# Grouped scaling of attention outputs, queries and keys stored by parts, operands of products 64 bytes apart

## The chip, the cores and the metric

The kernel runs on one core of a Trainium2 chip. The metric is the device time of one execution in microseconds; the median of three runs stands for a kernel. TensorE (PE in the profile) multiplies, VectorE (DVE), ScalarE (ACT) and GpSimd (POOL) do the element-wise work, SyncE (SP) issues most DMA transfers. PEld is TensorE's load of the stationary operand, which overlaps the multiplication.

## The reference

Two layers of a diffusion backbone. 2048 latent tokens and 256 context tokens of width 1024 go through one input projection, three groups of heads, one output projection, and a mixture of 16 experts of which each chooses its tokens. Group A is windowed attention (6 query heads on 2 key heads, with a sink in the softmax), group B a gated short convolution, group C neighbourhood attention of 6 heads on a grid with a bias by relative position.

```
qa, ka, va, bx, bb, bc, qn, kn, vn = _split_last(h @ w_in[l], IN_SPLITS)
...
p_win, p_ctx, _ = joint_softmax([s_win, s_ctx, s_sink])
o = (jnp.einsum('bnkgqj,bnjkd->bnqkgd', p_win.astype(v.dtype), vw)
     + jnp.einsum('bnkgqj,bjkd->bnqkgd', p_ctx.astype(v.dtype), v_ctx))
...
s_nb = s_nb + jnp.transpose(bias, (1, 0, 2, 3, 4))[None].astype(jnp.float32)
p_nb, p_ctx = joint_softmax([s_nb, s_ctx])
...
mix = jnp.concatenate([o_a, o_b, o_c], axis=-1) @ w_out[l]
...
y = jnp.einsum('becf,efd->becd', jax.nn.silu(a) * u, w_down) * gate[..., None].astype(h.dtype)
```

All of it is float32. The kernel splits each operand into a high and a low part and adds three products (high by high, low by high, high by low).

## The kernel before

Each layer runs four phases one after the other: `phase_in` (input projection), `phase_att` (attention), `phase_out` (output projection, LayerNorm, router) and `phase_moe` (experts). Within a phase the instructions of all engines are written in the order of the program; the order of attention is a string of steps per member (`ORDERA`, `ORDERC`) in the loop over `mem`, with the epilogue of a block (`pv`, a generator) advanced a step at every "R". Loads of weights (L163) run ahead as a stream on SP.

Products outside attention: L627 to L629 and L805 to L807 in the input phase, L1317 in the output phase, L1828 to L1830 (gate, up) and L1865 to L1867 (down) with the experts. Where a tile lies in SBUF is set by the order in which pools are opened. The distance of the two operands' addresses in a partition, modulo 128 bytes, is 96 for L627 to L629, 32 for L805 to L807 and for L1317, 96 (layer 0) and 64 (layer 1) for L1828 to L1830, 64 (layer 0) and 32 (layer 1) for L1865 to L1867, and mostly 0 for the products of attention (L1061, L1062, L1166).

The input phase writes queries and keys to DRAM, high and low part, by head: QA, QC, KC as [head, part, 64, tokens], KA as [head, part, 64, tokens] for two heads. One SBUF tile of 128 partitions holds two heads, so every store is made in two halves of 64 partitions (L660, L749, L787, L788).

Attention works unit by unit: two A units (a key head each) and six C units (a head each). An A unit has 18 blocks in layer 0 and 16 in layer 1, of three members (the query heads); a C unit has four blocks of four members, and in layer 0 before them a short one (n = 4) of two members for the context. Per member: logits (L1061, L1062, PE), maximum and mask (L1083, DVE), exponential (L1091, ACT), transposes (PE) with copies (L1220, ACT; L1211, DVE), and per block the product with the values (L1166, PE). The epilogue of a block: copy (L1172, ACT), in A the sink's share (L1174 DVE, L1175 ACT, L1184 DVE), transposes (L1179), copy (L1182), reciprocal (L1186), sum (L1188), scaling (L1191, all DVE), and stores to MIXA (one) or MIXC (four, L1199).

SP issues for attention, in order: the key load of the next unit (`load_unit`, L951; in A units with the fifth block, in C units with the second; at the phase's start in two parts of 640 and 1664 columns), with it the values va or vx and, for C, toep (L964), from which POOL builds the bias tiles (L1025); three query loads for each block, three blocks ahead (L976, L980, L982); four value loads for each C block, two blocks ahead (L994); and the stores. Keys of one head lie together: high and low part, 128 rows of 9216 bytes, one behind the other, go to 128 partitions. toep reads 8 x 16 rows of 4032 bytes.

Of the kernel before, what the change touches and what calls it, by code (L numbers as in the profile page):

```python
# [7 lines left out]
F32 = mybir.dt.float32  # L8
F32R = mybir.dt.float32r
BF = mybir.dt.bfloat16  # L10
I32 = mybir.dt.int32
AF = mybir.ActivationFunctionType
# [9 lines left out]
TT = SEQ + CTX  # L22
# [202 lines left out]
def build(ctx, tc, t, out):  # L225
# [4 lines left out]
    const = ctx.enter_context(tc.tile_pool(name="const", bufs=1))  # L230
    dram = ctx.enter_context(tc.tile_pool(name="dram", bufs=1, space=DRAM))
# [10 lines left out]
    half = const.tile([128, 2], F32, name="half")  # L242
# [9 lines left out]
    slotc = const.tile([128, 2], F32, name="slotc")  # L252
# [18 lines left out]
    QA = dr("QA", [6, 2, 64, TT])  # L271
    KA = dr("KA", [2, 2, 64, TT])
    QC = dr("QC", [6, 2, 64, TT])
    KC = dr("KC", [6, 2, 64, TT])
# [230 lines left out]
    def phase_in(l):  # L505
# [5 lines left out]

        hT = {-1: [hp.tile([128, KD, 512], F32R, name=z) for z in ("hh", "hl")]}
# [102 lines left out]
        def gemm(c):  # L615
# [16 lines left out]
            def c_rest(f, pg):  # L632
# [25 lines left out]
                for a, z in enumerate((sh, sl)):  # L658
                    for b in range(2):
                        SY.dma_start(dst[2 * (f % 3) + b, a, :, tok + t0:tok + nt],  # L660
                                     z.bitcast(F32)[64 * b:64 * b + 64, t0:nt])
# [77 lines left out]
            def ctx_rest(f, pg):  # L739
# [7 lines left out]
                for a, z in enumerate((sh, sl)):  # L747
                    for b in range(2):
                        SY.dma_start((QA[l][2 * f + b] if f < 3 else KA[l][b])[a, :, 0:256], z.bitcast(F32)[64 * b:64 * b + 64])  # L749

            def a_rest(i, pg):
# [32 lines left out]
                for a, o in enumerate((qh, ql)):  # L784
                    for b in range(2):
                        z = o.bitcast(F32)[64 * b:64 * b + 64]
                        SY.dma_start(QA[l][b::2, a, :, tk].rearrange("f p n -> p f n"), z[:, 0:3, :])  # L787
                        SY.dma_start(KA[l][b, a, :, tk], z[:, 3, :])  # L788
# [107 lines left out]
    def phase_att(l):  # L896
        es = ExitStack()

        kp = es.enter_context(tc.tile_pool(name="at_k", bufs=2))
        qp = es.enter_context(tc.tile_pool(name="at_q", bufs=1))  # L900
        vwp = es.enter_context(tc.tile_pool(name="at_vw", bufs=3))
        op = es.enter_context(tc.tile_pool(name="at_o", bufs=6))
        mp = es.enter_context(tc.tile_pool(name="at_m", bufs=1))
        vp = es.enter_context(tc.tile_pool(name="at_v", bufs=2))
        sm = es.enter_context(tc.tile_pool(name="at_s", bufs=4))
        pp = es.enter_context(tc.tile_pool(name="at_p", bufs=3))
# [11 lines left out]
        biases = [None, bp.tile([128, BWID], F32, name="bias")]  # L918
# [11 lines left out]
        NM = len(mem)  # L930
# [1053 lines left out]
```

## Time and profile before

| | us |
|---|---|
| median of three runs | 4121.46 (4118.05 to 4125.27) |
| profiled execution | 4118.59 |
| its span | 4116.8, mean granted clock 0.960 |
| busy PE, DVE, ACT, POOL | 3801.8, 2899.2, 2007.7, 706.6 |

The page of the profile gives busy time and shares by engine, the groups of instructions by line, and the transfers; a window gives the same for a stretch; the timeline gives single instructions with their starts. Matmuls overlap, so that the mean of one in a group is longer than the step from one to the next; the step is read from the timeline.

### The profile page before, as it was taken

What the parts mean: (1) busy time and instruction counts of PE and PEld (TensorE: products, weight loads), DVE (VectorE), ACT (ScalarE), POOL (GpSimd) and SP (SyncE); (2) the same over time, 40 slices, a digit from 0 to 9 for tenths busy, and PEclk for the clock granted to TensorE, in tenths of its full rate; (3) what the DMA queues carried; (4) which work ended last, traced back from release to release, by engine and by line L of the source; (5) the groups of instructions that cost most, each with busy time, mean ns of one, the idle gap of its engine ahead of it and who ended that gap; (6) DMA issues with size and microseconds to landing.
All of it is one profiled execution on the core that took longest, in us unless ns stands there. A gap on an engine that the chain in (4) does not pass through costs nothing. (4 is left out here: it accounts for less than half of the span.)

```text
span 4116.8 us, 64178 instructions
## 1 busy us (share of the span) xinstructions
PE 3801.8 (92%) x22980; PEld 3241.1 (79%) x22980; DVE 2899.2 (70%) x5836; ACT 2007.7 (49%) x3918; POOL 706.6 (17%) x658
## 2 busy tenths in 40 slices
PE   7999999999898899999996999989998966999983
PEld 5877788888787378989985888888897855999972
DVE  6555558999677467767756766469996776777765
ACT  4344337988433044444434434359884332444453
POOL 0000000022123023233311000000221221222214
PEclk9999999999999999999998999999999977999996
DMA  7566665377643677777757766563676424888875
GB/s 227 172 201 206 191 191 143 94 177 175 216 162 122 201 246 219 218 217 216 209 164 225 228 196 188 171 166 107 149 177 225 162 105 153 243 248 255 248 240 184
DMA packets 768951, 785.81 MB, mean 191 GB/s; under 512 B 144912, under 2 KB 650520, under 8 KB 766584
## 3 DMA queue, kind: packets, MB, share of 16 engines
q1 hardware_dynamic: 732776, 657.53, 53.3%
q0 software_dynamic: 34704, 123.13, 10.8%
q8 instruction: 182, 2.98, 0.3%
q14 instruction: 137, 1.12, 0.1%
q10 hardware_dynamic: 1152, 1.05, 0.1%
HBM read 603.05 MB, written 178.48 MB: 190 GB/s over the span
## 5 line engine op out<-in xcount | busy, mean ns | idle before, releaser
L178 ACT CAST wh<-wraw 128x1024 fp32r<-128x1024 f32 x636 | 657.9, 1051 | 387.5 <-DMA wraw<-in_w_in 116.5
L186 DVE TENSOR_TENSOR wl<-wraw,wh 128x1024 fp32r<-128x1024 f32 x636 | 751.2, 1216 | 19.2 <-ACT wh L178 18.8
L1211 DVE TENSOR_TENSOR pl<-pt,ph 128x256 fp32r<-128x256 f32 (+2 forms) x792 | 360.7, 495 | 13.0 <-ACT ph L1220 7.9
L627 PE MATMUL gem<-hh,wh 128*128 128x512 f32 (+1 forms) x960 | 354.5, 369 | 0.0
L628 PE MATMUL gem<-hl,wh 128*128 128x512 f32 (+1 forms) x960 | 352.2, 367 | 0.0
L1091 ACT ACTIVATE p<-lg,mx 128x640 f32<-128x640 f32 (+3 forms) x408 | 332.0, 814 | 37.7 <-DVE mx L1083 36.4
L629 PE MATMUL gem<-hh,wl 128*128 128x512 f32 (+1 forms) x960 | 350.4, 365 | 0.0
L1220 ACT CAST ph<-pt 128x256 fp32r<-128x256 f32 (+2 forms) x792 | 309.5, 446 | 59.1 <-PE pt L1108 53.3
L1828 PE MATMUL pu<-xh,wh 128*128 128x288 f32 (+1 forms) x1024 | 304.6, 297 | 10.1 <-DVE sa L1656 10.1
L1828 PE MATMUL pa<-xh,wh 128*128 128x288 f32 (+1 forms) x1024 | 300.9, 294 | 0.9 <-DVE modc L419 0.9
L1061 PE MATMUL lg<-k,q 128*128 128x384 f32 (+2 forms) x768 | 280.1, 387 | 20.9 <-DMA maskA<-in_maskA 7.4
L1830 PE MATMUL pa<-xh,wl 128*128 128x288 f32 (+1 forms) x1024 | 296.9, 290 | 0.8 <-DVE wl L186 0.8
L1830 PE MATMUL pu<-xh,wl 128*128 128x288 f32 (+1 forms) x1024 | 296.4, 289 | 0.0
L1829 PE MATMUL pa<-xl,wh 128*128 128x288 f32 (+1 forms) x1024 | 294.4, 288 | 0.0
L1829 PE MATMUL pu<-xl,wh 128*128 128x288 f32 (+1 forms) x1024 | 294.1, 287 | 0.0
L1567 POOL DMA_INDIRECT xe<-H,ix x80 | 164.7, 2059 | 473.3 <-DVE ix L1562 398.2
L1062 PE MATMUL lg<-k,q 128*128 128x256 f32 x816 | 228.3, 286 | 0.4 <-ACT p L1091 0.4
L1690 POOL DMA_INDIRECT ACC<-y,ix x62 | 127.1, 2050 | 583.6 <-DVE y L1671 324.3
L1865 PE MATMUL py<-wh,gh 128*128 128x512 f32 x512 | 206.5, 403 | 17.3 <-ACT gh L1658 10.1
L805 PE MATMUL gem<-wh,hh 128*128 128x512 f32 x544 | 220.7, 406 | 0.0
L806 PE MATMUL gem<-wl,hh 128*128 128x512 f32 x544 | 217.3, 399 | 1.4 <-DVE wl L186 1.4
L807 PE MATMUL gem<-wh,hl 128*128 128x512 f32 x544 | 216.9, 399 | 0.0
(346 smaller groups left out, 9681.5 us busy)
## 6 DMA issues: line engine op xcount, KB each, us to landing
wraw<-in_w_in SPq DMA_DIRECT2D x160, 512.0 KB
wraw<-in_w_gate SPq DMA_DIRECT2D x128, 512.0 KB
wraw<-in_w_up SPq DMA_DIRECT2D x128, 512.0 KB
wraw<-in_w_down SPq DMA_DIRECT2D x128, 512.0 KB
wraw<-in_w_mod SPq DMA_DIRECT2D x88, 512.0 KB
vw<-VS SPq DMA_DIRECT2D x192, 128.0 KB
q<-QA SPq DMA_DIRECT2D x204, 96.0 KB
VS<-vs SPq DMA_DIRECT2D x36, 512.0 KB
```

Source lines behind the costliest of these rows:

```text
L178: self.nc.scalar.copy(h, self.raw[i])
L186: self.nc.vector.tensor_tensor(e[1], self.raw[i], e[0].bitcast(F32), op=ALU.subtract)
L627: P.matmul(pg[:, t0:nt], wh[:, cs_], hh[:, k, t0:nt], start=(k == 0), stop=False)
L628: P.matmul(pg[:, t0:nt], wh[:, cs_], hl[:, k, t0:nt], start=False, stop=False)
L629: P.matmul(pg[:, t0:nt], wl[:, cs_], hh[:, k, t0:nt], start=False, stop=(k == KD - 1))
L1061: P.matmul(pl[:, w0:512], q[:, x, m, :], win(k), start=(x == 0), stop=(x == 1))
L1091: S.activation(p[:, 0:768 - w0], rec["lg"][:, w0:768], AF.Exp, bias=st[b]["mx"][:, m:m + 1], scale=-1.0, accum_out=st[b]["ss"][:, m:m + 1])
L1211: V.tensor_tensor(view(st[b]["pl"]), src, view(st[b]["ph"].bitcast(F32)), op=ALU.subtract)
L1220: S.copy(view(st[b]["ph"]), src)
L1828: P.matmul(pp[f], wh[:, cs_], xh[:, kk, :], start=(kk == 0), stop=False)
L1829: P.matmul(pp[f], wh[:, cs_], xl[:, kk, :], start=False, stop=False)
L1830: P.matmul(pp[f], wl[:, cs_], xh[:, kk, :], start=False, stop=(kk == KD - 1))
```

## The change

First, the operands of the large products come to lie 64 bytes apart (modulo 128): small unused pools (`shift`) and a new order of the attention pools move the tiles, and the input phase drops a pair of tiles that it kept under index -1. Second, QA, QC, KC are laid out as [part, head, 64, tokens], and the two halves of a store become one transfer of 128 rows; queries are read from the new layout in the same shape. Third, the key loads: the two parts of a head now lie 884,736 elements (C) or 294,912 (A) apart, and the load's source is [2, 64, n]. Fourth, the outputs of up to four A blocks (two C blocks) go into one tile of 12 x 64 columns; sink's share, reciprocal and scaling are done once for the group, in A with the scaling on POOL, and the stores follow together: MIXA once per group, MIXC eight in a row. The reciprocal and the scaling of C stay on DVE. Two small constants share a tile.

On SP, in a C unit of layer 1 around the key load (k is the keys, q queries, vw and vx values; DMAHW0 to 7 are the eight lanes that a transfer must find free). Before:

```order
L951 DMA k<-KC_88 128x2304 [waits DMAHW1_49]
L958 DMA vx<-VS_90 128x2x128 [waits DMAHW2_49]
L964 DMA toep<-in_rpb 128x1x1008 [waits DMAHW3_49,Pool_49]
L1199 DMA MIXC_96<-o 8x16x64 [waits DMAHW4_49,DVE_49]
L1199 DMA MIXC_96<-o 8x16x64 [waits DMAHW5_49]
L1199 DMA MIXC_96<-o 8x16x64 [waits DMAHW6_49]
L1199 DMA MIXC_96<-o 8x16x64 [waits DMAHW7_49]
L982 DMA q_27373<-QC_86 64x8x64 [waits DMAHW0_49]
L982 DMA q_27373<-QC_86 64x8x64 [waits DMAHW1_49]
L982 DMA q_27373<-QC_86 64x8x64 [waits DMAHW2_49]
L994 DMA vw<-VS_90 32x8x128 [waits DMAHW3_49,PE_49]
```

After:

```order
L962 DMA k<-KC_87 128x1x2304 [waits DMAHW5_49]
L969 DMA vx<-VS_89 128x2x128 [waits DMAHW6_49]
L975 DMA toep<-in_rpb 128x1x1008 [waits DMAHW7_49,Pool_49]
L993 DMA q_26821<-QC_85 64x8x64 [waits DMAHW0_49]
L993 DMA q_26821<-QC_85 64x8x64 [waits DMAHW1_49]
L993 DMA q_26821<-QC_85 64x8x64 [waits DMAHW2_49]
L1005 DMA vw<-VS_89 32x8x128 [waits DMAHW3_49,PE_49]
L1005 DMA vw<-VS_89 32x8x128 [waits DMAHW4_49]
L1005 DMA vw<-VS_89 32x8x128 [waits DMAHW5_49]
L1005 DMA vw<-VS_89 32x8x128 [waits DMAHW6_49]
L1229 DMA MIXC_95<-o 8x16x64 [waits DMAHW7_49,DVE_49]
```

The stores that stood behind toep come later and in eights; q and vw stand right behind toep, and the third vw needs the lane of k. The key load's shape is now 128x1x2304, where it was 128x2304.

On DVE, one A block in the middle of a unit (lg logits, mx maximum, pl low part, ss sum, rs reciprocal, o output). Before:

```order
L1191 TENSOR_TENSOR o<-o,rs 128x192
L1174 TENSOR_TENSOR rs<-sinks,mx 128x3
L1211 TENSOR_TENSOR pl<-pt,ph 128x3x128
L1211 TENSOR_TENSOR pl<-pt,ph 128x2x128
L1083 ISA lg,mx<-lg,maskA,sinks 128x640
L1083 ISA mx 128x1
L1184 TENSOR_TENSOR ss<-ss,rs 128x3
L1211 TENSOR_TENSOR pl<-pt,ph 128x3x128
L1211 TENSOR_TENSOR pl<-pt,ph 128x2x128
L1186 RECIPROCAL rs<-ss 128x3
L1083 ISA lg,mx<-lg,maskA,sinks 128x640
```

After, the block that ends a group:

```order
L1191 TENSOR_TENSOR rs<-sinks,mx 128x12
L1241 TENSOR_TENSOR pl<-pt,ph 128x3x128
L1241 TENSOR_TENSOR pl<-pt,ph 128x2x128
L1097 ISA lg,mx<-lg,maskA,sinks 128x640
L1097 ISA mx 128x1
L1206 TENSOR_TENSOR ss<-ss,rs 128x12
L1241 TENSOR_TENSOR pl<-pt,ph 128x3x128
L1241 TENSOR_TENSOR pl<-pt,ph 128x2x128
L1209 RECIPROCAL rs<-ss 128x12
L1097 ISA lg,mx<-lg,maskA,sinks 128x640
L1097 ISA mx 128x1
L1211 TENSOR_TENSOR o<-pt,o 128x192
```

The scaling has left DVE, and L1174, L1184 and L1186 (now L1191, L1206, L1209) work on 12 columns once for four blocks; the three other blocks have only the sum (now L1211) of them. On POOL, from the start of attention in layer 0 to its first bias additions, after:

```order
L1217 TENSOR_TENSOR o<-o,rs 128x768 x4
L1217 TENSOR_TENSOR o<-o,rs 128x384
L1217 TENSOR_TENSOR o<-o,rs 128x768 x3
L1024 MEMSET bias 128x2048
L1028 MEMSET va 128x256 x3
L1036 TENSOR_TENSOR va<-maskC,toep 128x384
```

There the scaling stands alone, up to the first bias tiles.

The diff, with line numbers left out:

```diff
+
+    def shift(es, n):
+
+        pool = es.enter_context(tc.tile_pool(name="shift", bufs=1))
+        pool.tile([128, n // 4], F32, name="shift")
...
-    half = const.tile([128, 2], F32, name="half")
+    halves = const.tile([128, 4], F32, name="half")
+    half, slotc = halves[:, 0:2], halves[:, 2:4]
...
-    QA = dr("QA", [6, 2, 64, TT])
+
+    QA = dr("QA", [2, 6, 64, TT])
     KA = dr("KA", [2, 2, 64, TT])
-    QC = dr("QC", [6, 2, 64, TT])
-    KC = dr("KC", [6, 2, 64, TT])
+    QC = dr("QC", [2, 6, 64, TT])
+    KC = dr("KC", [2, 6, 64, TT])
...
-        hT = {-1: [hp.tile([128, KD, 512], F32R, name=z) for z in ("hh", "hl")]}
+        hT = {}
...
                 dst = QC[l] if f < 3 else KC[l]
                 for a, z in enumerate((sh, sl)):
-                    for b in range(2):
-                        SY.dma_start(dst[2 * (f % 3) + b, a, :, tok + t0:tok + nt],
-                                     z.bitcast(F32)[64 * b:64 * b + 64, t0:nt])
+                    SY.dma_start(dst[a, 2 * (f % 3):2 * (f % 3) + 2, :, tok + t0:tok + nt], z.bitcast(F32)[:, t0:nt])
...
-                    for b in range(2):
-                        SY.dma_start((QA[l][2 * f + b] if f < 3 else KA[l][b])[a, :, 0:256], z.bitcast(F32)[64 * b:64 * b + 64])
+                    SY.dma_start((QA[l][a, 2 * f:2 * f + 2] if f < 3 else KA[l][a])[:, :, 0:256], z.bitcast(F32))
...
-                    for b in range(2):
-                        z = o.bitcast(F32)[64 * b:64 * b + 64]
-                        SY.dma_start(QA[l][b::2, a, :, tk].rearrange("f p n -> p f n"), z[:, 0:3, :])
-                        SY.dma_start(KA[l][b, a, :, tk], z[:, 3, :])
+                    SY.dma_start(QA[l][a, :, :, tk].rearrange("(f b) p n -> (b p) f n", b=2), o.bitcast(F32)[:, 0:3, :])
+                    SY.dma_start(KA[l][a, :, :, tk], o.bitcast(F32)[:, 3, :])
...
         kp = es.enter_context(tc.tile_pool(name="at_k", bufs=2))
+        pp = es.enter_context(tc.tile_pool(name="at_p", bufs=3))
+        op = es.enter_context(tc.tile_pool(name="at_o", bufs=3))
+        shift(es, 64)
         qp = es.enter_context(tc.tile_pool(name="at_q", bufs=1))
-        vwp = es.enter_context(tc.tile_pool(name="at_vw", bufs=3))
-        op = es.enter_context(tc.tile_pool(name="at_o", bufs=6))
+        shift(es, 64)
+        bsp = es.enter_context(tc.tile_pool(name="at_bias", bufs=1))
+        tp = es.enter_context(tc.tile_pool(name="at_toep", bufs=2))
         mp = es.enter_context(tc.tile_pool(name="at_m", bufs=1))
         vp = es.enter_context(tc.tile_pool(name="at_v", bufs=2))
-        sm = es.enter_context(tc.tile_pool(name="at_s", bufs=4))
-        pp = es.enter_context(tc.tile_pool(name="at_p", bufs=3))
+        vwp = es.enter_context(tc.tile_pool(name="at_vw", bufs=3))
+        sm = es.enter_context(tc.tile_pool(name="at_s", bufs=3))
...
-        biases = [None, bp.tile([128, BWID], F32, name="bias")]
+        biases = [None, bsp.tile([128, BWID], F32, name="bias")]
...
+        group = {}
+        for kind, u in [("A", 0), ("A", 1)] + [("C", u) for u in range(6)]:
+            for rows in (range(2, 6), range(6, 10), range(10, 14), range(14, NT), (0, 1)) if kind == "A" else (
+                    ((4,), (0, 1), (2,), (3,)) if u == 5 else ((4,), (0, 1), (2, 3))):
+                for j, n in enumerate(rows):
+                    group[kind, u, n] = ((kind, u, rows[0]), j, len(rows))
...
-            src = (KA if kind == "A" else KC)[l][u].rearrange("a d n -> (a d) n")
+            src = (KA if kind == "A" else KC)[l][:, u]
...
-                SY.dma_start(k.bitcast(F32)[:, 128 * t0:128 * t1], src[:, 128 * t0:128 * t1])
+                SY.dma_start(k.bitcast(F32)[:, 128 * t0:128 * t1], src[:, :, 128 * t0:128 * t1])
...
-                tz = bp.tile([128, 16, 64], F32, name="toep", bufs=2)
+                tz = tp.tile([128, 16, 64], F32, name="toep")
...
-            for x, a, y in ((0, 0, 0), (0, 1, 0), (1, 0, 1)):
+            for x, a in ((0, 0), (0, 1), (1, 0)):
                 dst = q.bitcast(F32)[64 * a:64 * a + 64, x]
-                    SY.dma_start(dst[:, 0:3], QA[l][3 * u:3 * u + 3, y, :, 128 * n:128 * n + 128].rearrange("m d n -> d m n"))
+                    SY.dma_start(dst[:, 0:3], QA[l][x, 3 * u:3 * u + 3, :, 128 * n:128 * n + 128].rearrange("m d n -> d m n"))
-                src = QC[l][u][y]
+                src = QC[l][x, u]
...
-                st[b] = {z: sm.tile([128, 4], F32, name=z) for z in ("mx", "ss", "rs")}
+                g, j, ng = group[b]
+                if j == 0:
+                    st["of", g] = {z: sm.tile([128, 12], F32, name=z)[:, 0:ng * nm] for z in ("mx", "ss", "rs")}
...
-                V.tensor_tensor(rec["rs"][:, :nm], sink[:, 3 * u:3 * u + 3], rec["mx"][:, :nm], op=ALU.subtract)
-                S.activation(rec["rs"][:, :nm], rec["rs"][:, :nm], AF.Exp, scale=-1.0)
+            g, j, ng = group[b]
+            of = st["of", g]
+            end = j == ng - 1
+            if end and kind == "A":
+                V.tensor_tensor(of["rs"].rearrange("p (b m) -> p b m", b=ng),
+                                sink[:, None, 3 * u:3 * u + 3].to_broadcast([128, ng, 3]),
+                                of["mx"].rearrange("p (b m) -> p b m", b=ng), op=ALU.subtract)
+                S.activation(of["rs"], of["rs"], AF.Exp, scale=-1.0)
             yield
             px = pst.tile([128, 4, 128], F32, name="pt")
             for m in range(nm):
                 P.transpose(px[:, m, :], ot[:, 128 * m:128 * m + 128], ident)
             yield
-            o = op.tile([128, 4, 64], F32, name="o")
-            S.copy(o[:, :nm, :], px[:, :nm, 64:128])
+            if j == 0:
+                of["o"] = op.tile([128, 12, 64], F32, name="o")[:, 0:ng * nm, :]
+            all_ = of["o"]
+            o = all_[:, j * nm:j * nm + nm, :]
+            S.copy(o, px[:, :nm, 64:128])
+            if end and kind == "A":
+                V.tensor_tensor(of["ss"], of["ss"], of["rs"], op=ALU.add)
+            yield
+            if end:
+                V.reciprocal(of["rs"], of["ss"])
+            yield
+            V.tensor_tensor(o, px[:, :nm, 0:64], o, op=ALU.add)
+            del st[b], blks[b]
+            if not end:
+                return
+            yield
+            yield
+            (G if kind == "A" else V).tensor_tensor(all_, all_, of["rs"][:, :, None].to_broadcast([128, ng * nm, 64]),
+                                                       op=ALU.mult)
+            n0 = g[2]
             if kind == "A":
-                V.tensor_tensor(rec["ss"][:, :nm], rec["ss"][:, :nm], rec["rs"][:, :nm], op=ALU.add)
-            yield
-            V.reciprocal(rec["rs"][:, :nm], rec["ss"][:, :nm])
-            yield
-            V.tensor_tensor(o[:, :nm, :], px[:, :nm, 0:64], o[:, :nm, :], op=ALU.add)
-            yield
-            yield
-            V.tensor_tensor(o[:, :nm, :], o[:, :nm, :], rec["rs"][:, :nm, None].to_broadcast([128, nm, 64]), op=ALU.mult)
-            if kind == "A":
-                SY.dma_start(MIXA[l][128 * n:128 * n + 128, 192 * u:192 * u + 192], o[:, 0:3, :].rearrange("p m d -> p (m d)"))
+                SY.dma_start(MIXA[l][128 * n0:128 * (n0 + ng), 192 * u:192 * u + 192].rearrange("(b p) c -> p b c", p=128),
+                             all_.rearrange("p (b m) d -> p b (m d)", b=ng))
             elif n == 4:
-                SY.dma_start(MIXC[l][0:256, 64 * u:64 * u + 64].rearrange("(m p) d -> p m d", p=128), o[:, 0:2, :])
+                SY.dma_start(MIXC[l][0:256, 64 * u:64 * u + 64].rearrange("(m p) d -> p m d", p=128), all_)
             else:
                 dst = MIXC[l][256:TT, 64 * u:64 * u + 64].rearrange("(m a g b) d -> m g a b d", m=4, a=8, g=4)
-                for m in range(4):
-                    (G if b == blist[-1] else SY).dma_start(dst[m, n], o[:, m, :])
-            del st[b], blks[b]
+                for x in range(ng):
+                    for m in range(4):
+                        (G if b == blist[-1] else SY).dma_start(dst[m, n0 + x], all_[:, 4 * x + m, :])
+            del st["of", g]
...
+        if last:
+            shift(es, 32)
         sb = es.enter_context(tc.tile_pool(name="moe_sb", bufs=2))
+        shift(es, 96 if last else 32)
         one = es.enter_context(tc.tile_pool(name="moe_one", bufs=1))
```

## Rows read from the trace of the kernel before

**Rows 1.** The page, part 1: busy time of the engine, share, instructions.
```profile
PE 3801.8 (92%) x22980; PEld 3241.1 (79%) x22980; DVE 2899.2 (70%) x5836; ACT 2007.7 (49%) x3918; POOL 706.6 (17%) x658
```

**Rows 2.** Windows in an A and a C stretch: busy (instructions), PEclk, DMA share, GB/s.
```profile
core 0: us, PE busy (x) PEld busy (x) DVE busy (x) ACT busy (x) POOL busy (x), PEclk, DMA share, GB/s
660.00:720.00 60.00, 60.00 (x426) 55.20 (x425) 59.67 (x184) 55.16 (x163) 0.00 (x0) 1.00 0.39 115
2967.00:3000.00 33.00, 32.97 (x247) 30.01 (x246) 31.84 (x75) 28.75 (x72) 9.66 (x9) 1.00 0.79 181
```

**Rows 3.** Timeline of PE, down product, layer 0, then layer 1: start, duration, engine, line.
```profile
1492.84 0.39 PE L1865 MATMUL py<-wh,gh 128*128 128x512 f32 x1
...
1498.12 0.40 PE L1867 MATMUL py<-wh,gl 128*128 128x512 f32 x1
...
3690.28 0.39 PE L1865 MATMUL py<-wh,gh 128*128 128x512 f32 x1
...
3694.96 0.40 PE L1867 MATMUL py<-wh,gl 128*128 128x512 f32 x1
```

**Rows 4.** Groups by line and form: busy us, mean ns | idle before.
```profile
L627 PE MATMUL gem<-hh,wh 128*128 128x512 f32 (+1 forms) x960 | 354.5, 369 | 0.0
...
L805 PE MATMUL gem<-wh,hh 128*128 128x512 f32 x544 | 220.7, 406 | 0.0
...
L1317 PE MATMUL po<-wh,mh 128*128 128x512 f32 x544 | 177.9, 408 | 0.5 <-ACT mh L1302 0.5
```

**Rows 5.** Timeline of DVE over one A block of layer 0.
```profile
672.06 0.35 DVE L1191 TENSOR_TENSOR o<-o,rs 128x192 f32<-128x192 f32 x1
672.34 0.16 DVE L1174 TENSOR_TENSOR rs<-sinks,mx 128x3 f32<-128x3 f32 x1
672.41 0.88 DVE L1211 TENSOR_TENSOR pl<-pt,ph 128x384 fp32r<-128x384 f32 x2
...
674.00 0.16 DVE L1184 TENSOR_TENSOR ss<-ss,rs 128x3 f32<-128x3 f32 x1
...
675.00 0.17 DVE L1186 RECIPROCAL rs<-ss 128x3 f32<-128x3 f32 x1
...
677.74 0.36 DVE L1191 TENSOR_TENSOR o<-o,rs 128x192 f32<-128x192 f32 x1
```

**Rows 6.** Groups by line and form: the bias additions on POOL.
```profile
L1025 POOL TENSOR_TENSOR bias<-maskC,toep 128x384 f32<-128x384 f32 x36 | 36.8, 1022 | 125.2 <-DMA toep<-in_rpb 46.5 <-DVE mx L1083 46.2 <-DVE o L1191 22.8
```

**Rows 7.** Windows: a key load in flight, then a toep load in flight.
```profile
2961.50:2963.00 1.50, 1.50 (x14) 1.31 (x13) 1.48 (x5) 1.31 (x4) 0.00 (x0) 1.00 0.98 389
842.90:844.70 1.80, 1.80 (x16) 1.75 (x15) 1.70 (x4) 1.27 (x4) 0.00 (x0) 1.00 0.55 149
```

**Rows 8.** DMA issues of the whole run, KB each.
```profile
k<-KC SPq DMA_DIRECT2D x12, 1152.0 KB
```

**Rows 9.** Timeline of SP and of PE at the start of attention, layer 0.
```profile
623.26 0.60 SPq L951 DMA_DIRECT2D k<-KA  x1
...
628.32 0.55 PE L1061 MATMUL lg<-k,q 128*128 128x256 f32 x1 [7.07 <-DMA k<-KA]
```

**Rows 10.** Timeline of SP in C units of layer 1, from key load to key load.
```profile
2924.97 0.45 SPq L951 DMA_DIRECT2D k<-KC  x1
...
2952.51 1.97 SPq L982 DMA_DIRECT2D q<-QC  x3
...
2958.26 0.45 SPq L951 DMA_DIRECT2D k<-KC  x1
...
2962.81 6.64 SPq L982 DMA_DIRECT2D q<-QC  x3
2970.10 1.80 SPq L994 DMA_DIRECT2D vw<-VS  x4
2972.00 2.48 SPq L1199 DMA_DIRECT2D MIXC<-o  x4
```

**Rows 11.** What SP waits for: us in total, times, longest.
```profile
SPq L982 <- DMA k<-KC: 8.6, 4, 4.8
```

More of the change, by code (lines that the diff above doesn't have):

```diff
@@ L251, in build @@
     sel = const.tile([128, 32], F32, name="sel")
-    slotc = const.tile([128, 2], F32, name="slotc")
     bits = const.tile([128, 15, 3], I32, name="bits")
@@ L1071, in soft_max @@
             if m == 0:
-                st[b] = {z: sm.tile([128, 4], F32, name=z) for z in ("mx", "ss", "rs")}
+                g, j, ng = group[b]
+                if j == 0:
+                    st["of", g] = {z: sm.tile([128, 12], F32, name=z)[:, 0:ng * nm] for z in ("mx", "ss", "rs")}
+                st[b] = {z: x[:, j * nm:j * nm + nm] for z, x in st["of", g].items()}
             first = 3e38
@@ L1180, in pv @@
             yield
-            o = op.tile([128, 4, 64], F32, name="o")
-            S.copy(o[:, :nm, :], px[:, :nm, 64:128])
-            if kind == "A":
-                V.tensor_tensor(rec["ss"][:, :nm], rec["ss"][:, :nm], rec["rs"][:, :nm], op=ALU.add)
+            if j == 0:
[5 more added lines that the diff above has]
+                V.tensor_tensor(of["ss"], of["ss"], of["rs"], op=ALU.add)
```

## The prediction

> **What bounds the kernel now.** The page's first lines say that PE is busy 92% of the span [rows 1]; the stretches say where that is a limit and where it is not. In a minute of A blocks (60 us of layer 0) PE and DVE are both full, 60.00 and 59.67 us of 60, ACT stands at 55.16 and POOL does nothing; in a C stretch PE fills 32.97 of 33 us, DVE 31.84, POOL 9.66 [rows 2]. In the large products (input, output, experts) PE runs matmul on matmul, so that there the number of matmuls times the distance from one start to the next is the time. SP only issues transfers; where it is late is told with part 4.
>
> **Part 1, operands 64 bytes apart.** The trace holds the comparison already. The down product of the experts (L1865 to L1867) has its two operands 64 bytes apart (modulo 128) in layer 0 and 32 apart in layer 1. In layer 0 a row of 24 matmuls starts from 1492.84 to 1498.12: 23 steps of 229.6 ns. In layer 1 21 start from 3690.28 to 3694.96: 20 steps of 234.0 ns [rows 3]. So 4.4 ns a matmul of 512 columns. With 32 bytes run, beside the layer 1 down product (half of 3 x 512), L805 to L807 (3 x 544) and L1317 (3 x 544) [rows 4]: 4,032 x 4.4 ns = 17.7 us. L627 to L629 (3 x 960, [rows 4]) are 96 apart, which no row pairs with 64: between nothing and 2,880 x 4.4 = 12.7 us, and I take half, 6. For the gate and up products of layer 0 (96 apart, narrower) I take 1 of at most 3. The attention products go from 0 to 64; in A blocks DVE hides what they gain, in C they have no pair in the trace: 0. Sum **-25 us**, bounds 0 and -33. It lies on the path, since PE is what these phases wait for.
>
> **Part 2, stores of queries and keys.** The two halves of a store become one, some 260 fewer issues on SP. During the input phases PE is the engine that is full, SP issues beside it, and the stored bytes are the same: 0.
>
> **Part 3, the scaling of four A blocks at once.** One A block lasts from one scaling multiply (L1191) at 672.06 to the next at 677.74, 5.68 us, with DVE busy all through [rows 5]. Out of it goes L1191, 0.28 us until the next start, to idle POOL; three quarters of L1174 (0.07 us until the next start) and of L1184 and L1186 (0.16 and 0.17 long, by their pipelining some 0.1 to 0.2 each in the sequence) go as well: 0.28 + 0.75 x 0.34 = 0.53 us. What is late next is ACT, 55.16 of 60 us, so 5.22 us a block at its present work [rows 2]: I take -0.46 us a block. With 68 blocks in all (36 and 32) **-31 us**; -14 if PE, which is full in the same stretch, yields only 0.2, and -36 if ACT gives way too. POOL gets one multiply of 768 elements for every four blocks; its adds of 384 elements take 1.02 us [rows 6], so some 2 us of 22, and only a store waits for it. In C the scaling stays on DVE, halved in number, beside a full PE: 0.
>
> **Part 4, the key loads.** This decides the sign. Before, the two parts of a head lay one behind the other, and a load was 128 rows on both sides. Now the parts lie apart, and its source in DRAM is 2 x 64 rows. No load of this shape is in the trace; two neighbours are. The key load as it is fills all queues: share 0.98, 389 GB/s [rows 7], 389/(16 x 0.98) = 24.8 GB/s for each busy engine. The toep load, whose source is 8 x 16 rows onto the same 128 partitions, runs at share 0.55 with 149 GB/s, with little beside it [rows 7]: half of the 16 engines, as many as its leading 8. By that pattern a leading 2 puts the key load on two engines. Its 1152 KB [rows 8] are 1.18 MB: 3.0 us on sixteen engines, 1.18 MB/(2 x 24.8) = 23.8 us on two. If a busy engine moves only 149/(16 x 0.55) = 16.9 GB/s, as in the toep stretch, it is 34.9 us. The ends are 3.0 and 34.9; I take 23.8, since the packets are those of the key load, and 26.5 from issue to landing (the first key load now needs 5.06 us from issue to the first matmul [rows 9], of which 320 KB at 389 GB/s are 0.8; that fixed part was partly queries, so I add 2.7 and not 4.2).
>
> The Trainium skill states the same as a rule ("DMA: Bandwidth & Descriptors", "Why a DMA increments its semaphore by 16 and not by 1"): the number of engines is the largest one up to 16 that divides the slowest dimension, leaving out dimensions of one, of both patterns. For 2 x 64 onto 128 that is two, against sixteen before. By that rule the toep load gets eight, and the share of 0.55 agrees; for two, no run here shows it yet.
>
> What it costs: SP issues in order, and each load waits for the one eight before it to land (the eight lanes in the rows of the section on the change). Behind a key load SP issues seven more and stands; already now the queries behind one take 6.64 us where three of them take 1.97 otherwise [rows 10], and 8.6 us in four waits of SP are put down to the key load [rows 11]. A C unit of layer 1 lasts from key issue to key issue, 2924.97 to 2958.26, 33.3 us [rows 10]. Its own issues are 1.80 (values), 2.48 (stores) and 1.97 (queries) a block, 25.0 for four, and 1.5 for k, vx and toep: 26.5, of which the seven behind the key load, some 4, and the key load itself are inside the 26.5 us of landing. So 22 + 26.5 = 48.5 us a unit: SP becomes the bound, +15.2. Five key loads of a layer stand in C units, and SP's lead of one block (8.3 us) is used up first: 5 x 15.2 - 8.3 = 68 us. In layer 0 a unit has a half block more (+4.2 us of work, +2.6 of issues): 5 x 13.6 - 8.3 = 60 us. In each of the two A units of a layer the next unit's key load is issued with the fifth block; the queries of the fourth block after that queue behind the keys, on the same two engines too, and land at about 28 us, while four blocks of 5.2 are 20.8: +7, four times in all, 28 us. At the start the first 320 KB take 6.6 us on two engines and not 0.8: +5.8 in each layer, 12. The second part (832 KB, 17 us) is issued some 4 us after the first has landed and is needed two blocks (11.4 us) on: +10, twice, 20. Sum **+187 us** (68 + 60 + 28 + 12 + 20). Lower end, if SP's stand is hidden by the loads ahead and only the landing counts: two engines still cost 60 in the A units, and some 3.5 x 10 in C, 95. Upper end, with 34.9 us a load: 11 more on ten C loads and four A loads, +154. With sixteen engines: 0.
>
> **The rest** (the constants in one tile, the order of pools) issues and waits for nothing new: 0.
>
> **The sum** is made against the profiled execution: 4118.59 us, its span 4116.8; the median of three runs is 4121.46, 0.07% above, which I leave. 4118.6 - 25 - 31 + 187 = **4250 us**.
>
> **The rivals.**
> A. The two parts of the source are spread over all sixteen engines after all. Then only gains are left: 4118.6 - 25 - 31 = 4063 us, faster. For it: the destination is still 128 partitions. Against: the toep load's is too, and it gets half. The sign turns at three to four engines: at L us of landing, C costs 10 x (L - 11.3) - 25, and all of the 56 us are gone at about L = 18.
> B. Two engines, but only the landing counts: prefetch (queries three blocks ahead, values two) covers SP's stand in C. 4118.6 - 56 + 95 = 4158 us. For it: next unit's keys are asked for three blocks (25 us) ahead. Against: SP would need 26.5 of 33.3 us even without the stand [rows 10].
> C. The two engines run at the toep stretch's pace, or toep, vx and stores that share them delay everything further: 4250 + 154 = 4404 at most, 4350 in the middle. For it: toep and the stores with leading 8 need those engines, too.
> D. The distance of operands is not what made 4.4 ns (the layers differ in columns of the neighbours): 25 us more, 4275, inside the forecast's range.
> E. The scaling brings nothing because PE is as full as DVE in A: 31 us more, 4281, also inside.
>
> **How the numbers follow.** Forecast (two engines, SP bound, with D and E as its spread; 4195 to 4330): 0.62. A: 0.10. B: 0.14. C: 0.14. The range leaves out A and the upper half of C, 0.17 or a little more: 4145 to 4345. 0.2% is 8 us, about what a measurement of this kernel can tell from none. Faster: A with a small tail of B, 0.11. Within 0.2%: 0.02. Slower: 0.87. The predicted time is 4250.
>
> **What the profile would show.** Right: key loads with the DMA share near 2/16 when nothing else moves; waits of SP on k of 10 us and more behind each key load of a C unit; idle PE in attention, some 80 to 100 us per layer, ended by toep, vw, q or k; A blocks of 5.2 us where no load is late, with POOL multiplies of 2 us; steps of 230 ns in L805 and L1317. Wrong: landing of k within 6 us (A), or k waits in SP without idle time on PE (B), or 234 ns still in L805 (D), or A blocks of 5.6 us (E).

## The result and the profile after

The changed kernel takes 4381.44 us (median of four, 4380.06 to 4384.11); the kernel before, on the same chip, 4121.16. The ratio is 1.0633 (interval 1.0618 to 1.0648): 260 us slower. Slower was forecast, but 4250 us, and 4345 as the upper end: the loss is twice the 131 us that were worked out.

All of it lies in attention. From the end of the input phase's last matmul to the end of the last one in `phase_att` the timeline of PE gives 433.5 and 397.7 us before (layer 0 and layer 1), 567.9 and 541.7 after: 278 us more. The rest of the span became 17 us shorter (3285.6 to 3268.7 us); the other phases gained, as was said.

The key load in flight, in two windows of the kernel after (columns as in rows 2); in the first, queries move beside it, in the second nothing else does:

```profile
3212.00:3222.00 10.00, 0.00 (x0) 0.00 (x0) 0.00 (x0) 0.00 (x0) 0.00 (x0) 0.50 0.15 56
3268.00:3278.00 10.00, 0.00 (x0) 0.00 (x0) 0.00 (x0) 0.00 (x0) 0.00 (x0) 0.50 0.13 53
```

All five engines stand still; in the second window the DMA share is 0.13 and 53 GB/s: two engines of sixteen (0.125), 26.5 GB/s each. The trace's packets say the same: of the 128 packets of 9216 bytes of one such load (issued at 3196.95) two at a time are in flight for 23.4 of 26.1 us. Before, the same load ran at 0.98 and 389 GB/s [rows 7]. The granted clock of PE in the stretch is 0.50, the lower of its two levels.

SP in one C unit of layer 1, from key load to key load (timeline of after):

```profile
3195.11 1.79 SPq L1005 DMA_DIRECT2D vw<-VS  x4
3196.95 0.56 SPq L962 DMA_DIRECT2D k<-KC  x1
3197.55 0.47 SPq L969 DMA_DIRECT2D vx<-VS  x1
3198.12 0.66 SPq L975 DMA_DIRECT2D toep<-in_rpb  x1
3198.83 25.76 SPq L993 DMA_DIRECT2D q<-QC  x3
3224.69 4.58 SPq L1005 DMA_DIRECT2D vw<-VS  x4
3229.36 4.94 SPq L1229 DMA_DIRECT2D MIXC<-o  x8
3234.35 1.97 SPq L993 DMA_DIRECT2D q<-QC  x3
...
3251.57 2.04 SPq L1005 DMA_DIRECT2D vw<-VS  x4
3253.65 0.56 SPq L962 DMA_DIRECT2D k<-KC  x1
```

The three queries behind toep take 25.76 us, where before they took 6.64 behind a key load and 1.97 elsewhere [rows 10]. It is the issues themselves that last, from the first query on (ns of one issue: min, median, max):

```profile
L993 SPq DMA_DIRECT2D q<-QC x3: 2971/10850/11855, 3198.8 to 3221.6; - x3
```

The unit lasts 56.7 us, from 3196.95 to 3253.65; before it was 33.3 [rows 10]. What waits for it meanwhile, on PE, POOL and DVE (timeline; in brackets the idle time before and what ended it):

```profile
3225.32 0.66 PE L1072 MATMUL lg<-k,q 128*128 128x384 f32 x1 [19.01 <-issue]
...
3229.19 3.25 POOL L1036 TENSOR_TENSOR bias<-maskC,toep 128x384 f32<-128x384 f32 x3 [46.31 <-DMA toep<-in_rpb]
...
3230.25 0.83 DVE L1097 CUSTOM_DVE_ANT_0 lg<-lg,bias 128x640 f32<-128x640 f32 x1 [23.31 <-POOL bias L1036]
```

PE starts the next unit's logits 28.4 us after the key load was issued, when the keys are there; 4 us later toep is, and 1 us behind it DVE has its first bias tile. And the place of the same matmul in the kernel before (timeline of before, its key load issued at 2958.26 [rows 10]):

```profile
2970.98 0.34 PE L1061 MATMUL lg<-k,q 128*128 128x384 f32 x1
```

Only 12.7 us lie between issue and use there. This is one of the numbers that the prediction had wrong, below.

A blocks, in a window without a late load (layer 0, after):

```profile
703.00:737.00 34.00, 34.00 (x243) 31.46 (x242) 32.76 (x85) 30.75 (x87) 2.95 (x2) 1.00 0.39 123
```

DVE fell from full [rows 2] to 32.76 of 34 us, POOL works, and PE is busy in all 34.00. The blocks still last 5.7 us.

### The profile page after: what moved, and what is told of

The parts are those of the page before. It is cut to its first block, busy times and chain, and to the rows that moved or that the text cites. A ratio compares the mean times of both kernels' runs of the same rounds, so it can differ in the third digit from the quotient of the medians.

```text
span 4378.3 us, 63371 instructions
## 1 busy us (share of the span) xinstructions
PE 3823.2 (87%) x22980; PEld 3276.9 (75%) x22980; DVE 2870.2 (66%) x5574; ACT 2001.6 (46%) x3868; POOL 734.1 (17%) x676
## 5 line engine op out<-in xcount | busy, mean ns | idle before, releaser
L1072 PE MATMUL lg<-k,q 128*128 128x384 f32 (+2 forms) x768 | 292.7, 401 | 214.8 <-issue 111.7
L1072 PEld LDWEIGHTS lg<-k,q 128*128 128x128 f32 x768 | 153.6, 200 | 235.6 <-issue 195.2
L1073 PE MATMUL lg<-k,q 128*128 128x256 f32 x816 | 237.1, 297 | 41.8 <-DMA q<-QC 33.3
L1097 DVE CUSTOM_DVE_ANT_0 lg<-lg,maskA,sinks 128x640 f32<-128x640 f32 (+2 forms) x204 | 171.2, 840 | 97.1 <-PE lg L1073 83.4
L805 PE MATMUL gem<-wh,hh 128*128 128x512 f32 x544 | 220.1, 405 | 0.5 <-ACT hh L601 0.5
```

The costliest lines, as they stand in the source:

```text
L1072: P.matmul(pl[:, w0:512], q[:, x, m, :], win(k), start=(x == 0), stop=(x == 1))
```

## The experiments

The theory at first: the key load on two engines makes all of the loss; the distances give some 19 us, about what the other phases showed (17); the grouped scaling gives nothing, since PE is full in A too. The rival: the new order on SP (stores in eights, queries and values right behind toep) holds a good part.

**The key load split, the rest as changed** (e1_split).

```diff
-                SY.dma_start(k.bitcast(F32)[:, 128 * t0:128 * t1], src[:, :, 128 * t0:128 * t1])
+                for a in range(2):
+                    SY.dma_start(k.bitcast(F32)[64 * a:64 * a + 64, 128 * t0:128 * t1], src[a, :, 128 * t0:128 * t1])
```

> The changed kernel with one edit: each key load is issued as two transfers of 64 rows (high part, low part), so that neither has a leading dimension of two. Theory (the load on two engines, through SP's queue, makes the whole loss; the rest of the change is worth what the phases outside attention gained, some 19 us): 4095 to 4110 us, attention back to 425 to 432 us in layer 0 and 395 to 401 in layer 1, SP's query issues behind a key load of 2 to 7 us, no idle PE of 10 us in a C unit. Rival (the new order on SP, stores in eights and queries right behind toep, holds a third or more of the loss): 4190 us or more, with C units of layer 1 still above 38 us.

Measured 4136.74 us (1.0035, 1.0021 to 1.0048). 245 us of the loss are gone, but not to 4100: C units of layer 1 last 35.2 to 40.4 us (here and below from a unit's first output copy, L1172 before, to the next unit's; 33.3 to 33.5 before), so the order on SP or the split itself still costs some 35. The stall there is 4 to 5 us of PE, ended by DVE, which waited for POOL's bias, which waited for toep.

**Parts two and four alone** (e2_layout): queries and keys by parts in the kernel before, key load from 2 x 64 rows.

```diff
-    KC = dr("KC", [6, 2, 64, TT])
+    KC = dr("KC", [2, 6, 64, TT])
...
-                SY.dma_start(k.bitcast(F32)[:, 128 * t0:128 * t1], src[:, 128 * t0:128 * t1])
+                SY.dma_start(k.bitcast(F32)[:, 128 * t0:128 * t1], src[:, :, 128 * t0:128 * t1])
```

> The kernel before with parts two and four alone: queries and keys stored by parts in merged stores, key loads from 2 x 64 rows; operand distances, epilogue and its stores as before. Theory: the whole loss is here, 4121 + 260 + 19 (no gain from distances) = 4385 to 4415 us, C units of layer 1 of 50 to 57 us. Rival (order of stores and queries holds a third or more): 4300 us or less.

Measured 4385.89 us (1.0648, 1.0632 to 1.0664). The loss is all there without groups and without distances.

**The distances alone** (e3_dist): the unused pools, the order of the attention pools, no tiles under index -1.

```diff
+        shift(es, 64)
         qp = es.enter_context(tc.tile_pool(name="at_q", bufs=1))
...
-        hT = {-1: [hp.tile([128, KD, 512], F32R, name=z) for z in ("hh", "hl")]}
+        hT = {}
```

> The kernel before with part one alone (small unused pools, order of the attention pools, no tiles under index -1, two constants in a tile). Theory: the phases outside attention gain what they gained in the changed kernel, 4098 to 4108 us, with steps of L805 and L1317 at 230 ns and attention unchanged within 3 us a layer. The prediction's term was -25 us: 4096. Rival (the distance is not what makes 4.4 ns): 4121 us within 4.

Measured 4099.28 us (0.9948, 0.9934 to 0.9962): -20.5 us, the theory's time. But not by the steps that were named. The output product, before (L1317) and in this kernel (L1325), then the input product of this kernel (L809 to L811, which were L805 to L807), on PE's timeline:

```profile
1085.47 0.63 PE L1317 MATMUL po<-wh,ml 128*128 128x512 f32 x2
...
1088.27 0.63 PE L1317 MATMUL po<-wh,ml 128*128 128x512 f32 x2
```

```profile
99.39 0.39 PE L810 MATMUL gem<-wl,hh 128*128 128x512 f32 x1
...
105.93 0.39 PE L811 MATMUL gem<-wh,hl 128*128 128x512 f32 x1
...
1084.80 0.62 PE L1325 MATMUL po<-wh,ml 128*128 128x512 f32 x2
...
1090.30 0.62 PE L1325 MATMUL po<-wh,ml 128*128 128x512 f32 x2
```

L1317 went from 12 steps in 2.80 us, 233 ns, to 24 in 5.50, 229 ns. The input product, 28 steps in 6.54 us, stands at 233.6 ns with its operands 64 apart. Over the whole run the medians (start to start) are 234 to 229-231 ns for L1317, 234-235 to 233 for L805 to L807, 231, 237, 231 to 231, 226, 229 for L627 to L629 (512 columns), 120-121 to 118 (256 columns), and the down product of layer 1 went from 234 to 229-230. The down product of layer 0, 64 apart before and after, became longer, 229-231 to 232-233: the distance alone does not set the step.

**The groups alone** (e4_group): the new epilogue in the kernel before (one line of it here; the rest is as in the diff of the change).

```diff
+            (G if kind == "A" else V).tensor_tensor(all_, all_, of["rs"][:, :, None].to_broadcast([128, ng * nm, 64]),
+                                                       op=ALU.mult)
```

> The kernel before with part three alone: grouped sink's share, reciprocal, scaling and stores, scaling of A on POOL. Theory (PE is as full as DVE in A blocks, so that taking work from DVE gives nothing): 4121 us within 8, A blocks of 5.65 to 5.7 us, DVE idle 0.2 us before each block's copies. The prediction's term was -31 us: 4090, A blocks of 5.22. Rival (stores in eights cost SP time in C): 4130 or more with C units above 33.6 us.

Measured 4128.33 us (1.0021, 1.0012 to 1.0030), +8.6 us: the -31 us of the prediction do not exist. A blocks last 5.7 us, as before; attention of layer 0 became 1.6 us shorter, that of layer 1 7.5 us longer: in two C units (40.4 and 36.0 us) the key load came 5.5 and 5.2 us after the unit's first output copy, behind eight stores, where it came 2.2 and 3.5 us after it before. The time lies between the theory's upper end and the rival's lower one.

Two runs were to say what the split key load and the groups cost in the first one.

**Without groups, key load split** (e7_nogroup): the edit of the first run, with the epilogue of before.

> The changed kernel without part three (epilogue and stores per block as before) and with each key load in two transfers of 64 rows. Theory now: what the split kernel lost against 4099 comes from the grouped stores of C, which push the key load and with it toep back, past the few us of slack that the bias tiles have; without the groups 4098 to 4108 us, C units of layer 1 of 33.3 to 34 us. Rival (the split loads or the new layout cost it): 4120 to 4130 us, C units above 36 us.

Measured 4114.96 us (0.9985, 0.9976 to 0.9994), 16 above the distances alone: the expectation was wrong, and the rival nearer. SP and POOL of this kernel, then POOL of the kernel before for the same step (its toep was issued at 2959.29):

```profile
2989.37 1.12 SPq L956 DMA_DIRECT2D k<-KC  x2
...
2991.22 0.67 SPq L969 DMA_DIRECT2D toep<-in_rpb  x1
...
3003.75 3.17 POOL L1030 TENSOR_TENSOR bias<-maskC,toep 128x384 f32<-128x384 f32 x3 [26.74 <-DMA toep<-in_rpb]
```

```profile
2970.20 3.24 POOL L1025 TENSOR_TENSOR va<-maskC,toep 128x384 f32<-128x384 f32 x3 [22.82 <-DMA toep<-in_rpb]
```

With two half loads ahead of it toep is there 12.5 us after its issue, with one whole load 10.9. The landing events of the trace go with it: one load of 128 rows begins to land 4.9 to 5.7 us after issue, the second of two halves 7.7 to 8.2 after the first one's issue. Two us suffice to make DVE wait for bias tiles; the slack that looked large on POOL (22.82 us idle) is small on the chain. DVE's waits for them in layer 1's C units (us, times, longest), this kernel, then the kernel before:

```profile
DVE lg L1088 <- POOL bias L1030: 12.2, 3, 5.2
DVE lg L1088 <- POOL va L1030: 3.4, 2, 1.9
```

```profile
DVE lg L1083 <- POOL bias L1025: 0.3, 1, 0.3
```

That is about the 16 us.

**Groups in A alone, key load split** (e8_groupA).

```diff
-                    ((4,), (0, 1), (2,), (3,)) if u == 5 else ((4,), (0, 1), (2, 3))):
+                    ((4,), (0,), (1,), (2,), (3,))):
```

> The changed kernel with the key loads split and with groups in A alone (each C block a group of its own). Theory (groups cost in C and bring nothing in A): 4097 to 4108 us, A blocks of 5.7 us. Rival (the groups of A cost, by the scaling on POOL or by late stores): 4115 us or more.

Measured 4138.63 us (1.0047, 1.0033 to 1.0061). It doesn't answer the question: with every C block a group of its own and three output tiles, ACT now waits for the stores that free them (waits in attention of layer 1: us, times, longest):

```profile
ACT o L1205 <- DMA MIXC<-o: 27.3, 5, 6.4
```

**Key load issued by ScalarE** (e5_act), **by GpSimd** (e9_pool), to tell SP's standing from the landing.

```diff
-                SY.dma_start(k.bitcast(F32)[:, 128 * t0:128 * t1], src[:, :, 128 * t0:128 * t1])
+                S.dma_start(k.bitcast(F32)[:, 128 * t0:128 * t1], src[:, :, 128 * t0:128 * t1])
```

(GpSimd: G for S.)

> The changed kernel with the key loads as they are, 2 x 64 rows, but issued by ScalarE and not by SP. Theory (most of the loss is SP standing behind the key load, so that everything after it comes late): SP no longer stands, C units of layer 1 of 36 to 44 us, 4150 to 4230 us. Rival (the long landing on two engines itself, wherever it is issued, makes the loss): C units above 48 us, 4320 us or more.

Measured 4424.01 us (1.0737, 1.0720 to 1.0753), slower still. SP was not freed. Its timeline, and the key load on ACT's queue:

```profile
3262.22 33.98 SPq L1229 DMA_DIRECT2D MIXC<-o  x8
...
3270.81 0.51 ACTq L962 DMA_DIRECT2D k<-KC  x1
```

The load now starts when ACT, in order, reaches it, 18 us after vx and toep that it used to precede, and the last of eight stores on SP is issued only at 3295.6, when the keys have landed. The lanes are handed out in the order of the program over both queues, so that a store still waits for the key load eight places ahead of it (SP's waits from 3250 to 3300):

```profile
SPq L1229 <- DMA k<-KC: 28.5, 1, 28.5
```

So this run cannot tell SP's standing from the landing.

> The changed kernel with key loads as they are (2 x 64 rows) but issued by GpSimd through its own queue. Theory (SP standing behind the load, by its lanes and its full queue, makes most of the loss; landing itself takes as long): SP's queries behind a key load 2 to 5 us, C units of layer 1 of 34 to 42 us, 4170 to 4270 us. Rival (the landing on two engines itself, shared with queries, toep and values, makes it): C units above 48 us, 4330 us or more.

Measured 4340.07 us (1.0526, 1.0510 to 1.0542), the rival's side. In A it helped: the first A unit has no long block any more. In C not. The key load on POOL, SP's queries behind it, and the load's own time to land:

```profile
3136.04 0.83 POOL L962 DMA_DIRECT2D k<-KC  x1
...
3140.25 21.89 SPq L993 DMA_DIRECT2D q<-QC  x2
```

```profile
DMA to landing us min/median/max: 15.4/29.1/31.7
```

The keys are no longer in SP's queue, and two of its queries still take 21.89 us: it is not the keys' place in SP's own queue that holds them. I read it as a wait for the two busy engines, whoever issued the keys; no view shows what an issue waits for. Beside that the keys come later here: POOL reaches the load only behind bias additions that wait for toep, in the next unit 15 us after SP issued toep (3175.82 and 3190.46). The run does not part the two.

**The key load one block earlier** (e6_early), **half of C's stores left out** (e13_halfstores), **both** (e14_both): is a unit bound by late keys or by SP's issues?

```diff
-                if at == ustart[kind, u] + (4 if kind == "A" else 1) and x < len(ulist):
+                if at == ustart[kind, u] + (4 if kind == "A" else 0) and x < len(ulist):
...
-                    for m in range(4):
+                    for m in range(0, 4, 2):
```

> The changed kernel with the key load of the next C unit issued at the first block of a unit and not at the second. Theory (a C unit lasts as long as SP needs, landing of the key load plus the remaining issues, so that it does not matter where in the unit the load stands): 4381 us within 20. Rival (the load only comes too late): 8.3 us earlier in ten units, 4300 to 4320 us.

> The changed kernel with half of the stores of C blocks left out (members two and four are not written; the buffer is filled once at the start instead), so that SP issues 8 transfers less in each C unit, some 0.6 us each, 4.9 us a unit. Theory (a C unit lasts as long as SP stands behind the key load plus its other issues): 4.9 us less in each of the ten units that stand, 4381 - 49 = 4320 to 4345 us. Rival (the chain of key load, toep and bias alone sets the unit, SP's other issues lie beside it): 4370 to 4385 us.

> The changed kernel with both edits: half of the stores of C blocks left out (members two and four are not written; the buffer is filled once at the start instead), and the key load issued at the first block of a C unit. Theory now (two bounds of a C unit lie close together: the keys land some 27.5 us after issue where PE asks for them 12.7 us after it in layer 1, and SP stands behind the load and then catches up; lifting one leaves the other): more than the sum of the single gains (30 and 15), 4381 - 60 to -110 = 4270 to 4320 us, C units of layer 1 of 44 to 49 us. Rival (the two gains are independent pieces of one bound): 4330 to 4340 us.

Measured 4351.02 us (-30), 4366.52 us (-15), 4343.09 us (-38). None hit. But the two runs that leave stores out pay for filling the buffer at the start (timeline of the one with half the stores):

```profile
5.73 7.32 POOL L287 DMA_DIRECT2D MIXC<-ident  x6 [2.52 <-DMA ident<-in_ident]
```

The last matmul of layer 0's input phase ends at 634.9 (half the stores) and 634.5 us (both edits), in the changed kernel at 614.3. In attention alone, taken as in the section on the result (one profiled execution of each), the gains are 30, 30 and 56 us: nearly the sum, two pieces that add up, and not one bound behind the other. By layers (0 and 1) the early key load gives 2 and 28 us, the stores left out 20 and 10, both 16 and 40: in layer 1 late keys weigh most, in layer 0 SP's issues. With both edits the units of layer 1 from the second on last 47.7 to 49.3 us, about the 44 to 49 that were expected and below those of either edit alone (49.1 to 54.4, 50.9 to 54.0), while those of layer 0 stay at 49 to 59. PE's wait in the run with both edits, and SP before it:

```profile
3205.33 0.66 PE L1075 MATMUL lg<-k,q 128*128 128x384 f32 x1 [12.55 <-DMA q<-QC]
```

```profile
3178.76 18.07 SPq L1232 DMA_DIRECT2D MIXC<-o  x4
3196.88 6.36 SPq L996 DMA_DIRECT2D q<-QC  x3
```

It is no longer the keys that come last but queries, which SP issues only after it has stood in four stores. How much of a unit each of the waits (keys, queries, toep, SP's issues) would cost alone stays open.

**The keys alone as before** (e11_keysback): everything of the change but the layout and loads of keys.

```diff
-            src = (KA if kind == "A" else KC)[l][:, u]
+            src = (KA if kind == "A" else KC)[l][u].rearrange("a d n -> (a d) n")
```

> The changed kernel with the keys alone laid out as before (by head, both parts together; their stores in halves, each key load 128 rows); queries by parts, distances and groups stay. Theory: the key layout makes the whole loss, and what is left is the sum of the two single edits, -20.5 (distances) and +8.6 (groups): 4109 us within 8. Rival (another part holds some of it): 4140 us or more.

Measured 4104.44 us (0.9957, 0.9944 to 0.9971). The key layout makes 277 us (4381.4 - 4104.4), the rest of the change is a gain.

**Distances and queries by parts** (e10_dist_q) and, with it, **groups in A with output tiles enough for C** (e12_best).

```diff
-                of["o"] = op.tile([128, 12, 64], F32, name="o")[:, 0:ng * nm, :]
+                of["o"] = (op.tile([128, 12, 64], F32, name="o") if kind == "A" else
+                           op.tile([128, 4, 64], F32, name="oc", bufs=6))[:, 0:ng * nm, :]
```

> Parts one and two without the keys and without part three: operand distances, queries by parts with merged stores, keys by head, epilogue per block. Theory (merged stores lie beside a full PE, 0; the split key loads cost 15 us by landing toep 2 us later): 4096 to 4103 us, as the distances alone. Rival (merged stores of queries cost): 4110 us or more.

Measured 4098.77 us (0.9944, 0.9931 to 0.9958): merged stores of queries are worth nothing, as said.

> Distances, queries by parts, keys by head, groups in A alone, C blocks with six output tiles of their own as before. Theory: -20.5 for the distances, some -5 in A (the long block behind a key load and the blocks at the units' ends), nothing in C: 4092 to 4100 us. The prediction's step for groups in A would make it 4068. Rival (groups in A cost through stores or POOL): 4106 us or more.

Measured 4093.78 us (0.9934, 0.9920 to 0.9947), the fastest of all, 28 us below the kernel before and 288 below the changed one. Groups in A give some 5 us (the two intervals overlap), at the units' ends and after a key load, where DVE had been late; inside a unit, nothing. From the run with the keys alone as before (groups in A and C) it differs in the groups and output tiles of C alone: the groups in C cost 10.7 us (4104.44 against 4093.78; the two intervals just touch), more than those in A bring.

## Why the prediction was wrong

| term | worked out | measured |
|---|---|---|
| distances | -25 | -20.5 (alone) |
| groups | -31 | +8.6 (alone), -5 in A alone, +10.7 in C |
| key loads | +187 | +277 (changed kernel less the one with keys as before) |

**The mechanism** was right in its first half: two engines for the load, at 26.5 GB/s each (24.8 were taken), 28.4 us from issue to use (26.5 were taken), SP standing behind it. Rival A, sixteen engines, is out by the share of 0.13. The Trainium skill's rule on the number of engines ("DMA: Bandwidth & Descriptors", "Why a DMA increments its semaphore by 16 and not by 1"), which gave two for this shape, agrees with that share. Of the 277 us between the two layouts of keys, 245 went when each load was cut into two of 64 rows.

Where and why SP stands was wrong. That "each load waits for the one eight before it to land" would hold it at the third value load behind the keys, the eighth transfer after them. In the unit shown it stood from the first query on, inside the issues. Waits for the key load were foreseen as 10 us and more in each C unit; SP's row for them at the value loads of C, in the whole run (us, times, longest; all five in layer 0), is

```profile
SPq L1005 <- DMA k<-KC: 21.1, 5, 5.0
```

The stand was about as long as worked out all the same, 27.7 us from the key load's issue to the end of the queries, but for another reason than the one given.

**Part 4, C units: 128 worked out, 198 measured.** Units of layer 1 grew from 33.3 us to between 50.4 and 56.4 (+103 over five), those of layer 0 from 37.5 to between 53.9 and 58.1 (+94 over five); with parts two and four alone it is +94 and +85. The step that failed is "So 22 + 26.5 = 48.5 us a unit", and with it two assumptions. "Of which the seven behind the key load ... are inside the 26.5 us of landing": the first query already stood, so that vw, four issues of 4.58 us, and everything behind fell after the landing; SP needed 29 us from there to the next key load (3224.69 to 3253.65), not 22. "SP's lead of one block is used up first": there was hardly a lead to use up, the first of the five units of layer 1 is already 17 us longer. Rival B's "next unit's keys are asked for three blocks (25 us) ahead" holds in layer 0 alone, where the first matmul with the new keys stood 25.4 to 26.4 us behind their load before; in layer 1 logits run ahead of the block that the order of the program names, and the keys are used 12.7 us after issue. That number could have been read from the trace of before, by looking for the first matmul with the new keys and not at the unit's length. In layer 0 the keys now land 27 to 29 us after issue and alone would have been 1 to 3 us late; there PE waits for queries, in the middle of that attention so:

```profile
1015.08 0.55 PE L1073 MATMUL lg<-k,q 128*128 128x256 f32 x1 [10.21 <-DMA q<-QC]
```

**Part 4, A units and start: 60 worked out, 86 measured.** Each of the four blocks that wait for queries is 16.0 to 18.0 us long in place of 5.7 (46 us in all, against 28). The first 320 KB cost 6.3 and 5.5 us more to the first matmul (11.4 and 10.9 us from issue), 5.8 each were worked out; the second part cost some 14 in each layer, not 10. (With the C units these pieces add to 284; blocks of A that got shorter take the rest back, to the 278 us of attention.)

**Part 3** failed in "what is late next is ACT, 55.16 of 60 us". PE stood at 60.00 of 60 in the same row. The prediction named the case (E), only as a spread of the forecast; it was the right one, and a bound that is full in a row is next before one that has 5 us left. The groups in C then cost what part 3 had put at 0: "In C the scaling stays on DVE, halved in number, beside a full PE" looks at DVE and PE alone, but the eight stores of a group stand ahead of the next key load.

**Part 1** was near in its sum, not in its pieces: the 4.4 ns of the down product carried over to L1317 (233 to 229) but only about 1 ns to L805 to L807, whose 7 us were lost, while L627 to L629 gave some 11 and not 6. A distance of 64 is not alone what makes a step short; what else does stays open.

**The range**: rival C, the same two engines with everything that shares them delayed further, came true in its second half, and the range cut it in the middle. That its time (4350 to 4404) holds the measured one is luck: it was worked out from 34.9 us of load on the engines, and the packets took 26.1.

## What to carry to other kernels

Where a load's two sides are cut differently, read its engines from the DMA share of a window in which nothing else moves, and before a layout is changed ask what the load's outermost dimension will be. A late load costs from the point where it is first used, which the trace shows (issue to first instruction that reads it), not where the program's loop puts it. When one engine is relieved, look at every engine that is full in the same window: the next bound may have no slack at all.

## What the runs showed of the hardware

- While a load on two DMA engines is in flight, the engine that issues the next transfers can stand in the issue itself. Single query issues of the changed kernel (ns: min, median, max) took up to 19.9 us, and two took 21.89 us even when the keys were in another engine's queue:

```profile
L993 SPq DMA_DIRECT2D q<-QC x144: 573/627/19876, 848.4 to 3352.3; - x144
```

- Two loads of 64 partitions landed later than one of 128 with the same bytes: the second of the two began to land 7.7 to 8.2 us after the first one's issue, the one load 4.9 to 5.7 us after its own.
- PE pays for a stall once more behind it. In the 19 us of a stall the granted clock is 0.58, in the 8.3 us after it 0.75, then 1.00 (0.50 and 1.00 are its two levels):

```profile
3206.00:3225.00 19.00, 0.31 (x3) 0.11 (x1) 0.94 (x4) 0.95 (x3) 0.00 (x0) 0.58 0.18 64
3225.30:3233.60 8.30, 6.96 (x35) 6.17 (x36) 3.35 (x8) 3.75 (x9) 4.41 (x5) 0.75 0.48 111
3233.60:3246.00 12.40, 12.40 (x94) 11.38 (x94) 11.74 (x29) 10.78 (x27) 5.29 (x5) 1.00 0.75 155
```
